# Mamba-2 SSD, two chunks: the second chunk's inter-chunk part from scores against the first chunk, instead of from a state

## The chip, the cores and the metric

The kernel runs on one core of a Trainium2 chip. The core has engines with a queue of instructions each: TensorE (PE; its weight loads are shown as PEld), VectorE (DVE), ScalarE (ACT), GpSimd (POOL) and SyncE (SP, which here only issues DMAs). The metric is the device time of one execution in microseconds (us), lower is better. A profile shows one execution of the program, recorded by the hardware.

## What is computed

The program is one decoder layer over 256 tokens of width 1024: a SwiGLU block, a mixer, another SwiGLU block. The mixer runs a Mamba-2 SSD branch and a retention branch side by side. The change lies in the SSD branch alone. Cut to it:

```python
CHUNK = 128                                   # 256 tokens: two chunks
SSD_N_HEADS, SSD_N_GROUPS = 32, 4             # 8 heads share B and C of a group
SSD_HEAD_DIM, SSD_D_STATE = 64, 128

def ssd_branch(z, xbc, dt_raw, ...):
    ...
    xdt = xs * dt[..., None]
    cb = jnp.einsum('bclgn,bcsgn->bgcls', cm, bm)
    scores = cb[:, :, None] * segsum_exp(a)
    y_diag = jnp.einsum('bgrcls,bcsgrp->bclgrp', scores, xdt)
    decay_to_end = jnp.exp(a_cs[..., -1:] - a_cs)
    chunk_states = jnp.einsum('bclgn,bgrcl,bclgrp->bcgrpn', bm, decay_to_end, xdt)
    chunk_decay = jnp.exp(a_cs[..., -1])
    prev_states = exclusive_chunk_scan(jnp.moveaxis(chunk_states, 1, 0), ...)
    y_off = jnp.einsum('bclgn,cbgrpn,bgrcl->bclgrp', cm, prev_states, jnp.exp(a_cs))
    y = y_diag + y_off + xs * d_skip.reshape(g_, r_)[..., None]
    ...
```

With two chunks only the second one has a `y_off`, and its `prev_states` is the state that the first chunk leaves behind.

## The kernel before

Activations lie transposed, features on the 128 partitions and the 256 tokens along the row. All weights come from memory in 1 MB stages (`wst`, four buffers, issued by SP in program order as buffers come free). Each stage is split into a rounded high half and the remainder: ACT casts the high half (L137), DVE subtracts (L138), into a ring of four buffers (`wh`). A projection multiplies high by high, high by low and low by high (`mm3`, L148 to L154), all in the reduced type f32r; these make nearly all of PE's work. The small products inside the branches are plain f32, which the trace shows as two instructions for each product and as one for each transpose.

The mixer is a list of steps, `ORDER` (L55), carried out in turn as program order. A planner takes this order as priority and lays the queue of each engine from its own estimates of durations; on DVE, ACT and SP neighbouring steps therefore mix. The SSD steps, for each of four groups `g`:

- `conv.8` to `conv.11` give B and C of all groups, `bT` and `cT` (state dimension on the partitions, tokens along the row). `conv.0` to `conv.7` give the inputs `xs`. The last `conv` in the order is `conv.3`.
- `bc` (`bc_products`, L658), once. Four transposes (L661) turn the first chunk's B; ACT copies them to `bn` (L662). Then eight products of 128 columns (L669), for each group and chunk that chunk's B against the same chunk's C; DVE multiplies them by the triangle and writes `cbm` (L672).
- `ml.g` (`mask_rows`) broadcasts the cumulated decays by POOL's DMAs into `m` and `ec`; `ma.g`, `mb.g` (`ssd_masks`) turn them into exponentials on ACT.
- `states.g` (`ssd_states`, L695) transposes `xs` (L700), scales it by dt into `xd` (L701), and scales the first chunk by its decay to the chunk's end into `xe` (L706).
- `mul.g` (`mask_scores`, L741) multiplies the masks by `cbm` (L743).
- `state.g` (`ssd_state`, L711) multiplies `bn` and `xe` to the state of the group, 128 x 512 (L715), and ACT copies it to `st` (L716).
- `back.g` (`ssd_back`, L746) does the products within chunks (L754), adds the skip (L760), then multiplies `st` by the second chunk's C (L764), scales by `ec` (L766) and adds (L767).

`v.p`, `z.g.p`, `bs.g.p`, `norma.g` and `normb.g` between them are projections and norms of the same mixer. PSUM tiles of the small products come from four buffers (`misc_ps`), those of projections from four others (`proj_ps`); each is one bank.

`xe`, `st` and `bn` are single buffers of 128 x 512, `ec` has two. In the retention part behind, `ret_scores` (L878) uses the same four names again for its decay masks, which SP loads (L881) when the buffer comes free.

Of the kernel before, what the change touches and what calls it, by code (L numbers as in the profile page):

```python
# [16 lines left out]
ALU = mybir.AluOpType  # L17

P = 128
T = 256  # L20
# [33 lines left out]

ORDER = (  # L55
# [27 lines left out]
def layer(ctx: ExitStack, tc: tile.TileContext, a, out, packing):  # L83
    nc = tc.nc
    pe, act, dve = nc.tensor, nc.scalar, nc.vector
# [12 lines left out]
    def nm(s):  # L98
        uid[0] += 1
        return f"{s}_{uid[0]}"  # L100

    def proj_ps():
        return pp.tile([P, 2, T], F32, tag="proj", name=nm("proj"))

    def misc_ps():
        return pm.tile([P, 512], F32, tag="misc", name=nm("misc"))
# [13 lines left out]
    def load(w, r0, nk, c0, ncol):  # L120
        st = stage()[:, :nk * ncol]
        fetch(st, w, lambda m: m[r0:r0 + nk * P, c0:c0 + ncol].reshape(nk, P, ncol)
              .transpose(1, 0, 2))
        return st.rearrange("p (k n) -> p k n", k=nk)
# [42 lines left out]
    ident = head[:, H_ID:H_ID + P]  # L167
    triu = k[:, K_TRI:K_TRI + P]
# [186 lines left out]
    with (tc.tile_pool(name="ep", bufs=1) as ep,  # L355
# [34 lines left out]
        for i in range(2):  # L390
# [8 lines left out]
            for f in range(2 - i):  # L399
                for tt in range(2):  # L400
                    pe.matmul(stat[:, tt * P:(tt + 1) * P], sq[:, f, tt * P:(tt + 1) * P], mean1,
                              start=i == f == tt == 0, stop=i == tt == 1, skip_group_check=True)
# [53 lines left out]
        ps = misc_ps()  # L456
        for c in range(2):
            pe.matmul(ps[:, c * P:(c + 1) * P], r[:, c:c + 1].broadcast_to([P, P]), ident,
                      start=True, stop=True)
# [84 lines left out]
    with tc.tile_pool(name="mx", bufs=1, reuse_waits="tile") as mx:  # L544
        def slot(shape, dt=F32, name="s"):
            return mx.tile(shape, dt, tag="slot", name=nm(name), bufs=SLOTS)
# [4 lines left out]
        def small(shape, tag, bufs=1):  # L551
            return mx.tile(shape, F32, tag=tag, name=nm(tag), bufs=bufs)
# [5 lines left out]
        bT, cT = slot([P, 4, T]), slot([P, 4, T])  # L558
# [84 lines left out]
        def silu_half(key, c0, p2):  # L643
            need("s")
            if p2 == 0:
                zs[key] = slot([P, 4, T])
            if key == ("z", 0):
                for f in range(4):
                    lookup(zs[key][:, f, :], first[f][0], AF.Silu, bias=first[f][1])
                return  # L650
            ps = pair_project(w_in, c0 + p2 * 256, u)
            lookup(zs[key][:, 2 * p2:2 * p2 + 2, :], ps, AF.Silu)

        bn = small([P, 512], "bn").rearrange("p (g n) -> p g n", g=4)
        cs, dend = small([P, 2, NH], "cs"), small([P, NH], "dend")
        cbs, states, masks = [], {}, {}

        def bc_products():  # L658
            ps = misc_ps()
            for g in range(4):  # L660
                pe.transpose(ps[:, g * P:(g + 1) * P], bT[:, g, :P], ident)  # L661
            act.copy(bn, ps.rearrange("p (g n) -> p g n", g=4))  # L662
            cbm = slot([P, 4, 2, P])
            for g2 in range(2):
                ps = misc_ps()
                for gg in range(2):
                    for c in range(2):
                        g = g2 * 2 + gg
                        pe.matmul(ps[:, (gg * 2 + c) * P:(gg * 2 + c + 1) * P],  # L669
                                  bT[:, g, c * P:(c + 1) * P], cT[:, g, c * P:(c + 1) * P],  # L670
                                  start=True, stop=True)
                dve.tensor_tensor(cbm[:, g2 * 2:g2 * 2 + 2].rearrange("p g c l -> p (g c) l"),  # L672
                                  ps.rearrange("p (a l) -> p a l", a=4),
                                  triu.unsqueeze(1).broadcast_to([P, 4, P]), ALU.mult)
            cbs.append(cbm)

        def decays():
# [30 lines left out]
                dend[:, 8 * g:8 * g + 8].unsqueeze(2).broadcast_to([P, 8, 64]), ALU.mult)  # L708
            states[g] = xd, xe

        def ssd_state(g):  # L711
            xd, xe = states[g]
            st = small([P, 512], "st")
            ps = misc_ps()
            pe.matmul(ps, bn[:, g, :], xe, start=True, stop=True)  # L715
            act.copy(st, ps)  # L716
            states[g] = xd, st

        def mask_rows(g):
            ec = small([P, 512], "ec", 2)  # L720
            m = [wide([P, 8, P]) for _ in range(2)]
            masks[g] = ec, m
            for c in range(2):
                nc.gpsimd.dma_start(m[c], rows[c:c + 1, 8 * g:8 * g + 8, :].broadcast_to([P, 8, P]))
            for hh in range(2):
                src = rows[1:2, 8 * g:8 * g + 8, :].rearrange("o (i two) l -> two o i l", two=2)[hh]
                nc.gpsimd.dma_start(ec[hh * 64:hh * 64 + 64, :].rearrange("p (i l) -> p i l", i=4),
                                    src.broadcast_to([64, 4, P]))

        def ssd_masks(g, c):  # L730
            need("e")
            ec, m = masks[g]
            for hl in range(8):
                hd = 8 * g + hl
                act.activation(m[c][:, hl, :], m[c][:, hl, :], AF.Relu,
                               bias=cs[:, c, hd:hd + 1], scale=-1.0)
            lookup(m[c], m[c], AF.Exp, scale=-1.0)
            if c == 1:
                lookup(ec, ec, AF.Exp)
# [4 lines left out]
                                  cbs[0][:, g, c, :].unsqueeze(1).broadcast_to([P, 8, P]), ALU.mult)  # L744

        def ssd_back(g):  # L746
            (xd, st), (ec, m) = states.pop(g), masks.pop(g)
            for f2 in range(2):
                py = misc_ps()
                for f in range(2):  # L750
                    for hh in range(2):
                        hl = (f2 * 2 + f) * 2 + hh
                        for c in range(2):
                            pe.matmul(py[hh * 64:hh * 64 + 64, f * T + c * P:f * T + (c + 1) * P],  # L754
                                      xd[:, c, hl * 64:hl * 64 + 64], m[c][:, hl, :],
                                      start=True, stop=True)
                for f in range(2):
                    ff = f2 * 2 + f
                    i = 4 * g + ff
                    dve.scalar_tensor_tensor(xs[g][:, ff, :], xs[g][:, ff, :], dskip[:, i:i + 1],  # L760
                                             py[:, f * T:(f + 1) * T], ALU.mult, ALU.add)
            po = misc_ps()
            for f in range(4):
                pe.matmul(po[:, f * P:(f + 1) * P], st[:, f * P:(f + 1) * P], cT[:, g, P:],  # L764
                          start=True, stop=True)
            dve.tensor_tensor(ec, ec, po, ALU.mult)  # L766
            dve.tensor_tensor(xs[g][:, :, P:], xs[g][:, :, P:],  # L767
                              ec.rearrange("p (f l) -> p f l", f=4), ALU.add)
# [139 lines left out]
        def ret_norm(hd):  # L908
# [14 lines left out]

        steps = {
            "dt": dt_tile, "conv": conv, "decays": decays, "bc": bc_products,
            "z": lambda g, p2: silu_half(("z", g), C_Z + g * 512, p2),
            "g": lambda g, p2: silu_half(("g", g), C_G + g * 512, p2),
            "states": ssd_states, "state": ssd_state,
            "ma": lambda g: ssd_masks(g, 0), "mb": lambda g: ssd_masks(g, 1), "ml": mask_rows,
            "mul": mask_scores, "back": ssd_back, "norma": norm_a,  # L930
            "normb": norm_b, "v": v_tile, "bs": lambda g, q: branch("s", "w_br_ssd", g, q),
            "br": lambda g, q: branch("r", "w_br_ret", g, q),
# [31 lines left out]
    with tc.tile_pool(name=nm("fp"), bufs=1, reuse_waits="tile") as fp:  # L964
# [5 lines left out]
        for p2 in range(NF // 2):  # L970
# [14 lines left out]
            if p2 == 5:  # L985
                g = sp.tile([P, KD], F32, tag="g", name=nm("g"), bufs=2)
# [4 lines left out]
                for q in range(2):  # L991
                    ps = misc_ps()
                    pe.matmul(ps, ones, diag[:, 4 * q:4 * q + 4, :].rearrange("p f t -> p (f t)"),
                              start=True, stop=True)
                    act.copy(gb[:, q * 512:(q + 1) * 512], ps)
            if p2 == 6:
                for tt in range(2):
                    for q in range(2):
                        ps = misc_ps()
# [17 lines left out]
        for bi in range(2):  # L1017
            c0, per, split = bi * 512, 4, NF - 6 if bi else NF
            ps = [proj_ps().rearrange("p f t -> p (f t)") for _ in range(2)]
# [6 lines left out]
            for k0 in range(0, NF, per):  # L1026
                kn = min(per, NF - k0)
                st = load("ffn2_w_out", k0 * P, kn, c0, 512)
# [82 lines left out]
```

## Time and profile before

| what | value |
|---|---|
| device time, median of 3 runs | 828.91 us (828.78 to 828.99) |
| device time of the profiled execution | 828.89 us |
| its span, first to last instruction | 826.8 us |
| instructions | 15886 |
| mean granted TensorE clock | 0.998 |
| DMA | 193.08 MB, 234 GB/s on the mean |
| first and last start of `bc`'s products (L661, L669) | 275.9 and 278.0 us |
| first and last start of the state products (L715) | 290.0 and 370.7 us |
| last start of L764 | 396.1 us |

Times inside a profile count from the span's start. A line such as L715 is the line of the kernel that issued the instruction. "Busy" is the share of the span in which an engine had an instruction under way. In the chain of the work that ended last, each piece of time is given to the instruction that the end waited for. A wait names what the engine was released by. Matmuls of PE are pipelined: the duration shown for one is longer than the distance to the next.

### The profile page before, as it was taken

Reading aid. Unit: us, or ns where it says so; the run is one execution under the profiler, and the core shown is the slowest. Engines: PE = TensorE matmul, PEld = TensorE weight load, DVE = VectorE, ACT = ScalarE, POOL = GpSimd, SP = SyncE. Lnnn points to the kernel's source line nnn. Section 1 sums busy time; section 2 is a strip of 40 time slices with the busy share of each in tenths; the row PEclk is TensorE's granted clock in tenths of the full one; section 3 lists DMA queues with packets and bytes.
Section 4 is the critical chain, followed back from the end, with each engine's and each line's share of the span. In section 5 each row is a group of like instructions: output and inputs, shape, how many; then the busy total and the mean of one; then the engine's idle time right before and its main releaser. Section 6 shows DMA issues by size and latency. Waiting matters only on the chain.

```text
span 826.8 us, 15886 instructions
## 1 busy us (share of the span) xinstructions
PE 816.1 (99%) x6612; PEld 787.0 (95%) x6612; DVE 666.9 (81%) x999; ACT 511.0 (62%) x731; POOL 10.3 (1%) x21
## 2 busy tenths in 40 slices
PE   8999999999999999999999999999999999999996
PEld 7999999999999989999999999999999999999885
DVE  7999899977989988787898778977979985455464
ACT  6566454556898777765565569765568754545342
POOL 0000000000200010000000000000000000000000
PEclk9999999999999999999999999999999999999999
DMA  9998899855685465546657754654565695455521
GB/s 367 415 418 344 314 349 366 335 180 173 233 309 200 158 216 187 200 130 239 229 182 301 254 205 153 211 198 171 212 218 183 255 360 185 176 185 185 206 87 52
DMA packets 30299, 193.08 MB, mean 234 GB/s; under 512 B 3458, under 2 KB 4098, under 8 KB 9619
## 3 DMA queue, kind: packets, MB, share of 16 engines
q1 hardware_dynamic: 28370, 186.07, 61.6%
q0 software_dynamic: 1568, 5.28, 1.9%
q8 instruction: 52, 0.85, 0.4%
q10 hardware_dynamic: 288, 0.72, 0.3%
q14 instruction: 21, 0.16, 0.1%
HBM read 190.97 MB, written 1.08 MB: 232 GB/s over the span
## 4 chain that ended last, share of the span: by engine, by line
PE 90%; ACT 3%; DVE 3%; DMA 3%; issue 1%; SPq 0%; ACTq 0%
PE proj L154 25%; PE proj L153 25%; PE proj L152 25%; PE proj L149 2%; PE proj L150 2%; PE proj L148 2%; DMA wst<-in_ffn_w_in_dram 2%; ACT wh L411 1%; DMA ada<-in_ada_w_dram 1%; PE misc L754 1%; PE misc L898 1%; PE misc L223 1%; DVE wh L414 1%; DVE wh L138 1%; DVE ada L197 1%; PE misc L764 1%
## 5 line engine op out<-in xcount | busy, mean ns | idle before, releaser
L138 DVE TENSOR_TENSOR wh<-wst,wh 128x1024 fp32r<-128x1024 f32 (+1 forms) x262 | 316.8, 1213 | 108.4 <-ACT wh L137 107.5
L137 ACT CAST wh<-wst 128x1024 fp32r<-128x1024 f32 (+1 forms) x262 | 272.4, 1042 | 171.0 <-PE proj L154 132.2
L152 PE MATMUL proj<-uh,wh 128*128 128x256 f32 (+1 forms) x1096 | 304.5, 278 | 0.0
L153 PE MATMUL proj<-ul,wh 128*128 128x256 f32 (+1 forms) x1096 | 303.2, 277 | 0.0
L154 PE MATMUL proj<-uh,wh 128*128 128x256 f32 (+1 forms) x1096 | 303.2, 277 | 0.0
L153 PEld LDWEIGHTS proj<-ul,wh 128*128 128x128 f32 x1096 | 205.8, 188 | 0.4 <-issue 0.2
L152 PEld LDWEIGHTS proj<-uh,wh 128*128 128x128 f32 x1096 | 205.8, 188 | 0.3 <-ACT wh L137 0.2
L154 PEld LDWEIGHTS proj<-uh,wh 128*128 128x128 f32 x1096 | 205.8, 188 | 0.2 <-issue 0.2
L152 PE MATMUL proj<-s,wh 128*128 128x256 f32 x312 | 87.1, 280 | 0.2 <-ACT s L142 0.2
L154 PE MATMUL proj<-s,wh 128*128 128x256 f32 x312 | 86.4, 277 | 0.0
L153 PE MATMUL proj<-s,wh 128*128 128x256 f32 x312 | 86.2, 277 | 0.0
L152 PEld LDWEIGHTS proj<-s,wh 128*128 128x128 f32 x312 | 58.5, 188 | 0.6 <-ACT s L142 0.4
L153 PEld LDWEIGHTS proj<-s,wh 128*128 128x128 f32 x312 | 58.6, 188 | 0.2 <-issue 0.2
L154 PEld LDWEIGHTS proj<-s,wh 128*128 128x128 f32 x312 | 58.6, 188 | 0.0
L197 DVE SCALAR_TENSOR_TENSOR ada<-ada,cb 128x1024 f32<-128x1024 f32 x48 | 57.3, 1219 | 0.0
L148 PE MATMUL proj<-uh,wh 128*128 128x256 f32 x152 | 42.0, 276 | 0.0
L149 PE MATMUL proj<-uh,wh 128*128 128x256 f32 x152 | 42.0, 276 | 0.0
L150 PE MATMUL proj<-ul,wh 128*128 128x256 f32 x152 | 42.0, 276 | 0.0
L152 PE MATMUL proj<-ah,wh 128*128 128x256 f32 x152 | 42.0, 276 | 0.0
L153 PE MATMUL proj<-al,wh 128*128 128x256 f32 x152 | 42.0, 276 | 0.0
L154 PE MATMUL proj<-ah,wh 128*128 128x256 f32 x152 | 42.0, 276 | 0.0
L186 ACT ACTIVATE s<-proj 128x512 f32<-128x512 f32 x33 | 19.7, 598 | 34.6 <-PE proj L154 32.5
(274 smaller groups left out, 1372.8 us busy)
## 6 DMA issues: line engine op xcount, KB each, us to landing
wst<-in_mix_w_in_dram SPq DMA_DIRECT2D x52, 1024.0 KB, 4.9
wst<-in_ffn_w_in_dram SPq DMA_DIRECT2D x43, 1024.0 KB, 5.5
wst<-in_ffn_w_out_dram SPq DMA_DIRECT2D x18, 1024.0 KB, 4.9
ada<-in_ada_w_dram SPq DMA_DIRECT2D x16, 1024.0 KB, 8.4
wst<-in_ada_w_dram SPq DMA_DIRECT2D x12, 1024.0 KB, 5.0
ada<-in_ada_w_dram SPq DMA_DIRECT2D x16, 512.0 KB, 12.6
wst<-in_w_br_ssd_dram SPq DMA_DIRECT2D x8, 1024.0 KB, 5.0
wst<-in_w_br_ret_dram SPq DMA_DIRECT2D x8, 1024.0 KB, 4.9
```

The source lines that it names most:

```text
L137: act.copy(hi, v)
L138: dve.tensor_tensor(lo, v, hi.bitcast(F32), ALU.subtract)
L148: pe.matmul(o, l[1], r[0], start=False, stop=False, skip_group_check=skip)
L149: pe.matmul(o, l[0], r[0], start=False, stop=False, skip_group_check=skip)
L150: pe.matmul(o, l[0], r[1], start=False, stop=False, skip_group_check=skip)
L152: pe.matmul(o, l[0], r[0], start=first, stop=False, skip_group_check=skip)
L153: pe.matmul(o, l[0], r[1], start=False, stop=False, skip_group_check=skip)
L154: pe.matmul(o, l[1], r[0], start=False, stop=last, skip_group_check=skip)
L186: phase["uses"].append(act.activation(*args, **kw).ins)
L197: dve.scalar_tensor_tensor(st[:, i, :], st[:, i, :], 1.0, cb, ALU.mult, ALU.mult, accum_out=raw[:, j, f0 + i:f0 + i + 1])
L223: pe.matmul(ps[:, :T], mean, s, start=i == 0, stop=i == len(parts) - 1)
L411: act.copy(hw[0][j], wst[kt][:, j, :])
```

## The change

The state of the first chunk is no longer formed. For the second chunk, the sum over the state dimension is done first: `bc` multiplies the first chunk's B by C of both chunks in one product of 256 columns per group. Its first half is masked as before; its second half, unmasked, is copied by ACT to `ahead` (in the buffer and under the tag that `bn` had). The products of the second chunk's B with its own C are done in four more products of 128 columns. `back.g` then multiplies `xe` by `ahead` where it multiplied `st` by C. The transposes of B, their copy, the steps `state.g` and their copies are gone; the other steps keep their order.

```diff
 ORDER = (
...
-    "conv.7 conv.5 conv.3 ma.0 bc v.0 mb.0 states.0 mul.0 v.1 state.0 back.0 ml.2 v.2 ma.1 v.3 "
-    "states.1 mb.1 norma.0 v.4 state.1 normb.0 mul.1 z.1.0 z.1.1 back.1 ml.3 states.2 bs.0.0 state.2 "
-    "ma.2 norma.1 bs.0.1 mb.2 v.5 normb.1 mul.2 z.2.0 z.2.1 v.6 back.2 states.3 bs.1.0 state.3 ma.3 "
+    "conv.7 conv.5 conv.3 ma.0 bc v.0 mb.0 states.0 mul.0 v.1 back.0 ml.2 v.2 ma.1 v.3 "
+    "states.1 mb.1 norma.0 v.4 normb.0 mul.1 z.1.0 z.1.1 back.1 ml.3 states.2 bs.0.0 "
+    "ma.2 norma.1 bs.0.1 mb.2 v.5 normb.1 mul.2 z.2.0 z.2.1 v.6 back.2 states.3 bs.1.0 ma.3 "
...
-        bn = small([P, 512], "bn").rearrange("p (g n) -> p g n", g=4)
+        ahead = small([P, 512], "bn").rearrange("p (g l) -> p g l", g=4)
...
         def bc_products():
-            ps = misc_ps()
-            for g in range(4):
-                pe.transpose(ps[:, g * P:(g + 1) * P], bT[:, g, :P], ident)
-            act.copy(bn, ps.rearrange("p (g n) -> p g n", g=4))
             cbm = slot([P, 4, 2, P])
             for g2 in range(2):
                 ps = misc_ps()
                 for gg in range(2):
-                    for c in range(2):
-                        g = g2 * 2 + gg
-                        pe.matmul(ps[:, (gg * 2 + c) * P:(gg * 2 + c + 1) * P],
-                                  bT[:, g, c * P:(c + 1) * P], cT[:, g, c * P:(c + 1) * P],
-                                  start=True, stop=True)
-                dve.tensor_tensor(cbm[:, g2 * 2:g2 * 2 + 2].rearrange("p g c l -> p (g c) l"),
-                                  ps.rearrange("p (a l) -> p a l", a=4),
-                                  triu.unsqueeze(1).broadcast_to([P, 4, P]), ALU.mult)
+                    g = g2 * 2 + gg
+                    pe.matmul(ps[:, gg * T:(gg + 1) * T], bT[:, g, :P], cT[:, g, :],
+                              start=True, stop=True)
+                ps = ps.rearrange("p (g c l) -> p g c l", g=2, c=2)
+                dve.tensor_tensor(cbm[:, g2 * 2:g2 * 2 + 2, 0, :], ps[:, :, 0, :],
+                                  triu.unsqueeze(1).broadcast_to([P, 2, P]), ALU.mult)
+                act.copy(ahead[:, g2 * 2:g2 * 2 + 2, :], ps[:, :, 1, :])
+            ps = misc_ps()
+            for g in range(4):
+                pe.matmul(ps[:, g * P:(g + 1) * P], bT[:, g, P:], cT[:, g, P:],
+                          start=True, stop=True)
+            dve.tensor_tensor(cbm[:, :, 1, :], ps.rearrange("p (g l) -> p g l", g=4),
+                              triu.unsqueeze(1).broadcast_to([P, 4, P]), ALU.mult)
             cbs.append(cbm)
...
-        def ssd_state(g):
-            xd, xe = states[g]
-            st = small([P, 512], "st")
-            ps = misc_ps()
-            pe.matmul(ps, bn[:, g, :], xe, start=True, stop=True)
-            act.copy(st, ps)
-            states[g] = xd, st
...
         def ssd_back(g):
-            (xd, st), (ec, m) = states.pop(g), masks.pop(g)
+            (xd, xe), (ec, m) = states.pop(g), masks.pop(g)
...
             for f in range(4):
-                pe.matmul(po[:, f * P:(f + 1) * P], st[:, f * P:(f + 1) * P], cT[:, g, P:],
+                pe.matmul(po[:, f * P:(f + 1) * P], xe[:, f * P:(f + 1) * P], ahead[:, g, :],
                           start=True, stop=True)
...
-            "states": ssd_states, "state": ssd_state,
+            "states": ssd_states,
```

## The prediction

> **What bounds the kernel now.** I start with the page: busy time of each engine (part 1), then its chain of the work that ended last (part 4).
>
> ```profile
> PE 816.1 (99%) x6612; PEld 787.0 (95%) x6612; DVE 666.9 (81%) x999; ACT 511.0 (62%) x731; POOL 10.3 (1%) x21
> ...
> PE 90%; ACT 3%; DVE 3%; DMA 3%; issue 1%; SPq 0%; ACTq 0%
> ```
>
> PE (TensorE's matmuls) is busy for 99% of the span and makes 90% of the chain. Since matmuls are pipelined, "busy" alone proves little, so the next view is the list of waits of PE, over the whole run:
>
> ```profile
> PE misc L389 <- DMA crow<-in_c_dram: 2.6, 1, 2.6
> PE misc L898 <- DVE m L889: 0.6, 1, 0.6
> PE proj L442 <- ACT wh L411: 0.4, 1, 0.4
> PE proj L152 <- ACT s L142: 0.2, 1, 0.2
> ```
>
> Columns: total us, times, longest. Asked for 270 to 400 us alone, where the SSD steps that the diff touches lie, the same list is empty; L898 is in the retention part behind them. So a microsecond of PE work taken out of the SSD steps should move everything behind it forward. Whether the feeders could follow is read from windows over these steps. The columns are length, then busy us of PE, PEld, DVE, ACT, POOL, then granted clock, share and rate of the DMA.
>
> ```profile
> 276.00:283.60 7.60, 7.60 (x45) 6.61 (x44) 6.50 (x14) 4.31 (x7) 0.00 (x0) 1.00 0.51 169
> 279.00:300.00 21.00, 21.00 (x123) 17.15 (x122) 18.47 (x25) 15.06 (x23) 2.35 (x4) 1.00 0.53 176
> 300.00:340.00 40.00, 40.00 (x305) 36.69 (x304) 32.70 (x43) 32.47 (x54) 1.79 (x3) 1.00 0.55 189
> 340.00:390.00 50.00, 50.00 (x382) 46.38 (x381) 40.09 (x54) 32.28 (x39) 0.00 (x0) 1.00 0.55 191
> ```
>
> PE fills each window at full clock (1.00). From 279 to 390 us DVE is idle for 2.5 + 7.3 + 9.9 = 19.7 us, and ACT for more: room for a change of a few microseconds, though not much in the first window.
>
> **The change, part by part.** What a step costs on PE is read from the chain in order of time (start, us, what), because the chain puts pipelined matmuls end to end. An f32 product appears as two instructions (x16 for the eight products of L669); a transpose as one.
>
> ```profile
> 276.08 0.44 PE misc L661 x4
> 276.52 1.79 PE misc L669 x16
> ...
> 290.12 0.86 PE misc L715 x2
> ...
> 292.92 1.09 PE misc L764 x8
> ...
> 311.28 0.86 PE misc L715 x2
> ...
> 332.64 0.86 PE misc L715 x2
> ...
> 370.43 0.86 PE misc L715 x2
> ...
> 483.69 0.43 PE misc L886 x2
> ...
> 499.59 0.70 PE misc L898 x2
> ```
>
> *Removed on PE.* The four transposes of B: 0.44 us. The eight 128-column products of `bc`: 1.79. The four `state` products (one per group, 512 columns): 4 x 0.86 = 3.44. Together 5.67 us.
>
> *Added on PE.* Four f32 products of 256 columns (first chunk's B against C of both chunks) and four of 128 columns (second chunk). The 256-column price is L886, same types, same width: 0.43 us each, so 1.72. For 128 columns half of the L669 row: 1.79 / 2 = 0.90. Together 2.62 us. As many columns are streamed as L669 and the transposes streamed; `bc` alone gets 2.62 - 2.23 = 0.39 us longer.
>
> *Net on PE: 5.67 - 2.62 = 3.05 us less.* The ends of this term: the first 256-column product of a group may cost 0.70, like the first L898 (0.27 more), and the eight 128-column instructions 1.09, like L764 (0.19 more), which leaves 2.59 us of saving. On the other side stands the 0.7 us that the weight loads of L764 idle in four times without a named releaser: if that was `st` after all, the saving is 3.75. I do not take it, because `st` of group 0 is written at 291.56 + 0.59 = 292.15, before L764 begins:
>
> ```profile
> 291.56 0.59 ACT L716 COPY st<-misc 128x512 f32<-128x512 f32 x1
> ...
> 292.85 0.97 PEld L764 LDWEIGHTS misc<-s,st 128*128 128x128 f32 x8 [0.17 <-issue]
> ...
> PEld misc L764 <- issue: 0.7, 4, 0.2
> ```
>
> *Cross-check by start times*, group 0. The timeline gives starts:
>
> ```profile
> 289.73 0.39 PE L154 MATMUL proj<-wh,ul 128*128 128x512 f32 x1
> 289.96 1.02 PE L715 MATMUL misc<-xe,bn 128*128 128x512 f32 x2
> ...
> 290.90 2.02 PE L754 MATMUL misc<-m,s 128*64 128x128 f32 x32
> ...
> 360.68 0.39 PE L154 MATMUL proj<-wh,ul 128*128 128x512 f32 x1
> 361.00 2.02 PE L754 MATMUL misc<-m,s 128*64 128x128 f32 x32
> ```
>
> From the last projection to the first L754 take 290.90 - 289.73 = 1.17 us with the state product between; in group 2, where `state` doesn't stand there, 361.00 - 360.68 = 0.32. Difference 0.85, against 0.86 in the chain.
>
> *What is late next in that place.* With `state.0` gone and `bc` 0.39 longer, L754 of group 0 starts at 290.90 - 0.85 + 0.39 = 290.44. It needs the masked scores of `mul.0`:
>
> ```profile
> 286.48 2.36 DVE L743 TENSOR_TENSOR m<-m,s 128x1024 f32<-128x1024 f32 x2
> ```
>
> They are done at 288.84, so 1.6 us remain. The product with `xe` (L764, unchanged in number and shape) now reads `xe`, which DVE writes before `mul.0`, and `ahead`, written in `bc`: both long there. In the order string `states.1` follows `back.0`, and so on, so that the single `xe` buffer, now held until L764, delays nobody.
>
> *ACT and DVE.* Groups of instructions by shape, with total us and mean ns:
>
> ```profile
> L662 ACT COPY bn<-misc 128x512 f32<-128x512 f32 x1 | 0.6, 568 | 0.0
> ...
> L716 ACT COPY st<-misc 128x512 f32<-128x512 f32 x4 | 2.3, 584 | 0.0
> ...
> L832 ACT ACTIVATE s<-proj,col 128x256 f32<-128x256 f32 x8 | 3.4, 472 | 6.7 <-PE proj L154 6.7
> ...
> L672 DVE TENSOR_TENSOR s<-misc,k 128x512 f32<-128x512 f32 x2 | 1.4, 679 | 0.0
> ...
> L281 DVE TENSOR_TENSOR misc<-misc,rs 128x256 f32<-128x256 f32 x4 | 1.7, 426 | 0.0
> ```
>
> ACT loses 0.57 + 4 x 0.58 = 2.9 us and gets two 256-column copies at about 0.47: 1.96 us less. DVE has 2 x 0.68 = 1.36 and gets 2 x 0.43 + 0.68 = 1.54: 0.18 more. I cost both at nothing: PE covers them, as it covers these engines' idle time above. If the cover were gone, DVE's 0.18 would be the price.
>
> *The added wait.* In `bc` DVE and ACT now read two halves of the same PSUM bank. The kernel already has that case: in a conv pair both halves of the bank are read by ACT (L571) and DVE (L574).
>
> ```profile
> L571 ACT ACTIVATE cv<-proj,col 128x256 f32<-128x256 f32 x24 | 13.3, 570 | 5.2 <-DVE cv L574 4.3 <-PE proj L154 0.9
> ```
>
> ACT waited there for DVE for 4.3 us in all, though the halves differ: the two readers are kept apart. So each copy to `ahead` will stand behind DVE's multiply of its bank, and behind it on ACT the last conv pair's activations and casts. From 276 to 283.6 ACT is idle for 7.60 - 4.31 = 3.3 us, which takes 2 x 0.47 - 0.57 = 0.37 us more and a wait. The Trainium skill, "PSUM — Partial Sum Buffer", section "PSUM bank collisions raise a hardware error", speaks against this part of the change: ScalarE and VectorE may not touch one bank's quadrant at once, two reads included. By that rule two readers gain nothing over one, and the first rival holds; the trace agrees with the 4.3 us.
>
> *Queues.* No DMA is added. The retention mask loads (L881) reuse `xe`, `st`, `bn`. `xe` and `bn` now come free after the last L764 instead of the last L715, `st` at once. SP already waits in this place:
>
> ```profile
> 374.92 0.43 SPq L881 DMA_DIRECT2D bn<-in_dmask_dram  x1
> ...
> 396.42 0.33 SPq L881 DMA_DIRECT2D st<-in_dmask_dram  x1
> 396.84 0.38 SPq L118 DMA_DIRECT2D wst<-in_mix_w_in_dram  x1
> ...
> SPq L881 <- PE misc L764: 5.7, 1, 5.7
> ```
>
> SP held the next weight load for 5.7 us and PE shows no wait behind it. Two mask loads in place of one there cost about 0.4 us of SP time (0.33 to 0.43 each): nothing on PE. POOL's mask broadcasts (released by L754) come earlier with it.
>
> **Sum.** The profiled execution took 828.89 us (span 826.8 and 2.1 around it), 0.02 below the median of 828.91. 828.89 - 3.05 = **825.8 us** (-0.37%). Behind the SSD steps every wait of PE hangs on something that PE releases, so the 3 us should arrive.
>
> **The rivals.**
>
> *ACT held behind DVE in `bc`.* For it: the L571 row, and DVE busy for 6.50 of 7.60 us around `bc`. Were DVE to reach its second multiply only at the end of that backlog, 283.6, ACT's copies end at 284.5, and the exponentials for `mul.0` slip. Against: ACT has 3.3 us idle, `mul.0` has 1.6 us slack. It decides from a hold of about 1.6 us on `mul.0`; a hold of 2.6 us gives back 1.0: 826.8.
>
> *The queues behind are laid differently.* The order on DVE and ACT comes from a planner with its own estimates, and taking instructions out may change it far away. The place where this would bite is the one behind with a PE wait, L898 at 499 us, fed by ACT then DVE.
>
> ```profile
> L197 DVE SCALAR_TENSOR_TENSOR wst<-wst,cb 128x1024 f32<-128x1024 f32 x24 | 29.0, 1220 | 0.8 <-DMA wst<-in_ada_w_dram 0.8
> ...
> L178 ACT ACT_TABLE_LOAD x30 | 38.5, 1283 | 1.2 <-PEq L1080 0.7
> ```
>
> One pair of L197 moved ahead of L889 delays PE by 2 x 1.22 = 2.4 us: 828.89 - 3.05 + 2.44 = 828.3, no change to be seen. Against: both orders follow the same step list.
>
> *Slower.* The same place at a higher price: two pairs of L197 (4.88) and a table load (1.28) on the path ahead of L889 make 6.2 us, and 828.89 - 3.05 + 6.16 = 832.0. It decides from 3.05 + 1.66 = 4.7 us of added wait. Against: the wait there is 0.6 us today, and no other step is renamed or moved.
>
> **How the numbers follow.** About 0.2% (1.66 us) is what can be told from no change here. Forecast 825.8, chance 0.72, own range 825.1 (saving 3.75) to 826.3 (2.59), and a little either way for the rest of the order. ACT held behind DVE, 826.8: 0.09. Queues laid differently, 828.3: 0.12. Slower, 832.0: 0.07. The range 825.0 to 827.3 holds the first two, 0.81. Faster by over 0.2% are the first two: 0.81; same 0.12; slower 0.07.
>
> **What would show it.** Right: no L715 row; the chain's `bc` rows sum to about 2.6 us with eight instructions of 256 columns; PE's waits between 270 and 480 us still absent; the last L764 starts about 3 us earlier, and the matmuls of the end too. The first rival shows as a wait of PE's L754 for DVE or ACT in group 0; the others as a longer wait at L898, or new ones further on. The forecast is wrong if the 256-column products take clearly more than 0.43, or if a PE wait above a microsecond appears anywhere behind.

## The result and the profile after

The changed kernel took 826.08 us (median of 6 runs, 825.60 to 826.34), the kernel before 828.85 us (828.66 to 828.99): a ratio of 0.9966 with a 95% interval of 0.9954 to 0.9977, about 2.8 us less. Forecast were 825.8. The profiled execution took 825.60 us, with a span of 823.4.

The page of the changed kernel, busy time of each engine and the chain that ended last:

```profile
PE 812.7 (99%) x6600; PEld 785.3 (95%) x6600; DVE 666.5 (81%) x1000; ACT 508.7 (62%) x728; POOL 10.3 (1%) x21
...
PE 88%; DVE 4%; ACT 3%; DMA 3%; issue 1%; SPq 0%; ACTq 0%
```

PE is busy for 3.4 us less and still for 99% of the span. Of its list of waits (total us, times, longest) these are the three longest. Lines behind the change have moved by seven, so L891 is the former L898, with the wait of before; new is the wait of L442 for ACT's L430, in the first 50 us of the program. From 270 to 480 us the list is empty, as before:

```profile
PE misc L389 <- DMA crow<-in_c_dram: 2.3, 1, 2.3
PE misc L891 <- DVE m L882: 0.6, 1, 0.6
PE proj L442 <- ACT uh L430: 0.6, 1, 0.6
```

The chain in order of time (start, us, what) shows the shift grow step by step. L664 and L672 are the products of `bc`, L747 the former L754, L757 the former L764, L879 the former L886:

```profile
276.25 1.73 PE misc L664 x8
277.98 0.89 PE misc L672 x8
...
290.67 1.95 PE misc L747 x32
292.62 1.09 PE misc L757 x8
...
322.09 1.95 PE misc L747 x32
...
358.95 1.95 PE misc L747 x32
...
390.35 1.95 PE misc L747 x32
...
480.69 0.43 PE misc L879 x2
```

`bc` takes 1.73 + 0.89 = 2.62 us. Against the profile before, `bc` begins 0.17 later (276.25 for 276.08). The four L747 begin 0.31, 1.19, 2.12 and 3.00 earlier (before: 290.98, 323.28, 361.07 and 393.35): after the first one, each step is the missing state product, 0.88 to 0.93. From there the shift stays, 3.00 at the first retention scores (480.69 for 483.69). Some 0.3 us more come in between there and the end of the retention part, where ACT's pair of activations ahead of the merge starts at 609.72 instead of 613.06; why was not followed up.

So far everything is as forecast. What did not fit was the spread: 0.74 us between the six runs of the changed kernel, 0.33 between those of the kernel before beside them.

### The profile page after: what moved, and what is told of

It is laid out like the page before. It is cut to its first block, busy times and chain, and to the rows that moved or that the text cites. A ratio compares the mean times of both kernels' runs of the same rounds, so it can differ in the third digit from the quotient of the medians.

```text
span 823.4 us, 15854 instructions
## 1 busy us (share of the span) xinstructions
PE 812.7 (99%) x6600; PEld 785.3 (95%) x6600; DVE 666.5 (81%) x1000; ACT 508.7 (62%) x728; POOL 10.3 (1%) x21
## 4 chain that ended last, share of the span: by engine, by line
PE 88%; DVE 4%; ACT 3%; DMA 3%; issue 1%; SPq 0%; ACTq 0%
PE proj L154 25%; PE proj L153 25%; PE proj L152 25%; PE proj L150 2%; PE proj L149 2%; PE proj L148 2%; DMA wst<-in_ffn_w_in_dram 2%; ACT wh L411 1%; DMA ada<-in_ada_w_dram 1%; PE misc L747 1%; DVE wh L138 1%; PE misc L891 1%; DVE ada L197 1%; DVE wh L414 1%; PE misc L223 1%
## 5 line engine op out<-in xcount | busy, mean ns | idle before, releaser
L186 ACT ACTIVATE s<-proj 128x512 f32<-128x512 f32 x33 | 19.7, 597 | 34.1 <-PE proj L154 31.8
```

The lines of the kernel that those rows point to most:

```text
L186: phase["uses"].append(act.activation(*args, **kw).ins)
```

## The experiments

Two theories stood at the start. **PE's work**: the gain is the 3.05 us that PE no longer does. **Another engine or queue**: it is ACT's lost copies, or the new order of the queues and the earlier load into `st`. A third one came out of the first runs.

### The products put back, without the copies (e1)

```diff
-    "conv.7 conv.5 conv.3 ma.0 bc v.0 mb.0 states.0 mul.0 v.1 back.0 ml.2 v.2 ma.1 v.3 "
+    "conv.7 conv.5 conv.3 ma.0 bc v.0 mb.0 states.0 mul.0 v.1 state.0 back.0 ml.2 v.2 ma.1 v.3 "
...
+        def ssd_state(g):
+            xd, xe = states[g]
+            ps = misc_ps()
+            pe.matmul(ps, ahead[:, g, :], xe, start=True, stop=True)
```

> The changed kernel with four idle products of 512 columns (first chunk's scores against xe, into a PSUM tile that nobody reads) at the places where the state products stood; no copy by ACT. If the gain is PE's work alone, the four products cost 4 x 0.86 = 3.44 us again: 826.08 + 3.44 = 829.5. If the gain came from the copies that ACT lost, or from the order of the queues and the earlier mask load, they cost nothing: 826.1.

Measured: 829.16 us (828.76 to 830.63, 11 runs), ratio to the kernel before 1.0005 (0.9996 to 1.0014). The chain of e1 has the four products again:

```profile
290.78 0.86 PE misc L715 x2
...
311.94 0.86 PE misc L715 x2
...
333.31 0.86 PE misc L715 x2
...
371.10 0.86 PE misc L715 x2
```

Matmuls that nobody reads give back the whole gain: 3.1 us above the 826.08, 3.5 above the 825.70 of the repeat below, for 3.44 expected (both on other chips; on its own chip e1 is 0.2 us slower than the kernel before, where 0.39 us of longer `bc` are left). That is PE's work, and speaks against the other theory. Of the 1.9 us between e1's lowest and highest run only 0.6 lie within the span (826.8 to 827.4); what the rest outside it is was not tried.

### The copies put back, without the products (e2, twice)

```diff
-    ... mul.0 v.1 back.0 ...
+    ... mul.0 v.1 state.0 back.0 ...
...
+        def ssd_state(g):
+            xd, xe = states[g]
+            act.copy(small([P, 512], "st"), xe)
```

> The changed kernel with four copies of 128x512 on ACT, xe to st, at the places where ACT copied the state; no product on PE. The buffer st is thereby held again until late, so that its mask load moves back too. If the gain is PE's work alone: 826.1, no change against the changed kernel. If it came from ACT: 4 x 0.58 = 2.3 us more, 828.4. If it came from the early mask load: above 826.1 by what that was worth.

Measured: 827.08 us (825.74 to 828.47, 11 runs), 0.9980 (0.9971 to 0.9989). Inconclusive: the lowest run is what PE's work gives, the highest what ACT's copies would cost, and the profiled run (826.27) has no wait of PE in the SSD steps.

### The kernel before, without the products (e5)

```diff
-            ps = misc_ps()
-            pe.matmul(ps, bn[:, g, :], xe, start=True, stop=True)
-            act.copy(st, ps)
+            act.copy(st, xe)
```

> The kernel before without its four state products: ACT copies xe to st in their place, so the second chunk's inter-chunk part is left wrong by the missing product with B. Transposes, bc, copies and buffers as before. If PE's work alone counts: 828.85 - 3.44 = 825.4. If it is ACT's copies that counted: 828.9.

Measured: 826.71 us (825.96 to 828.04, 11 runs), 0.9976 (0.9967 to 0.9984): 2.2 us of 3.44, with a wide spread again. Here the profile has the missing part. First the wait of PE, then its chain:

```profile
PE misc L223 <- DVE sql L776: 1.0, 1, 1.0
```

```profile
307.43 0.95 ACT wh L137
308.40 1.23 DVE wh L138
309.63 0.67 DVE s L701 x2
310.30 0.44 issue
310.74 0.68 DVE xe L706
311.43 0.35 DVE sql L776
311.81 0.38 PE misc L223
```

PE stands for 1.0 us before the norm's sum (L223), because ACT and DVE are late: with the state product gone, PE arrives earlier than they do. Why they are late is read from what ACT waits for; e5's chain itself shows mask activations between the casts and goes back from there to PE (at 302.65 us), not to the rows. The list of ACT's waits from 276 to 420 us, before and then after the change (L728 is the former L735, the first mask activation):

```profile
ACT m L735 <- DMA m<-rows: 4.0, 2, 3.0
```

```profile
ACT m L728 <- DMA m<-rows: 6.8, 2, 5.5
```

The planner has queued mask activations of later groups early on ACT, and there they stand for the broadcast of the mask rows, with weight casts and PSUM evacuations in order behind them. Each line sums two waits. The first ends near 300 us, 3.0 us long before the change and 5.5 now. The second ends near 329 us; before the change it was 1.0 long:

```profile
329.71 1.57 ACT L735 ACTIVATE m<-m,cs 128x128 f32<-128x128 f32 x5 [1.00 <-DMA m<-rows]
```

Hence a third theory, **ACT held by the mask rows**: PE's work gives the gain, and executions in which the rows land late give part of it back.

### The same kernel again, and the mask activations held back (a_again, e6)

```diff
-        act.copy(hi, v)
+        last["cast"] = act.copy(hi, v).ins
...
+            with tc.issue_after(last["cast"]) if g >= 2 else nullcontext():
                 for hl in range(8):
...
                     act.activation(m[c][:, hl, :], m[c][:, hl, :], AF.Relu,
```

> The changed kernel as it is, on the chip of the three kernels beside it. PE's work alone: 825.8, with the spread of the kernel before (some 0.6 us between lowest and highest). If a wait on ACT for the mask rows (5.5 us in the profile) now sometimes reaches PE: the same lowest time, but a spread of 1 us or more and a median above 826.

> The changed kernel; the mask activations of groups 2 and 3 may not be queued on ACT ahead of the weight cast that precedes them in the step list, so that ACT's casts no longer stand behind a wait for the mask rows' DMA. If that wait eats part of the gain in some executions: median 825.4 to 825.8 and a spread of 0.6 us or less. If PE's work alone decides: the same median and spread as the changed kernel, about 826.0.

Measured on one chip: the changed kernel 825.70 us (825.62 to 825.85, 5 runs), e6 825.60 us (825.54 to 825.68, 5 runs), the kernel before 828.77; 0.9964 (0.9951 to 0.9977) and 0.9962 (0.9949 to 0.9975). ACT's timeline in e6 (start, us, engine, line; in brackets what ended its idle time) has no wait for the rows; casts come with PE, the mask activations in one piece of eight:

```profile
297.89 1.05 ACT L139 CAST wh<-wst 128x1024 fp32r<-128x1024 f32 x1 [3.73 <-PE proj L156]
...
319.11 2.44 ACT L731 ACTIVATE m<-m,cs 128x128 f32<-128x128 f32 x8
```

The spread falls from 0.23 to 0.14 us. But the changed kernel's spread was small on this chip too, which by the expectation of a_again speaks for PE's work alone; e6 fits both of its answers. This pair alone decides nothing.

### One reader for each bank (e3), and the order within `back` (e4)

The edit of e3, in place of the products of `bc`:

```diff
+            for bc_, cc in ((0, 0), (0, 1), (1, 1)):
+                ps = misc_ps()
+                for g in range(4):
+                    pe.matmul(ps[:, g * P:(g + 1) * P], bT[:, g, bc_ * P:(bc_ + 1) * P],
+                              cT[:, g, cc * P:(cc + 1) * P], start=True, stop=True)
+                ps = ps.rearrange("p (g l) -> p g l", g=4)
+                if bc_ == cc:
+                    dve.tensor_tensor(cbm[:, :, cc, :], ps, ..., ALU.mult)
+                else:
+                    act.copy(ahead, ps)
```

> The changed kernel, with the products of bc laid into three PSUM banks that have one reader each: DVE for the first chunk's scores, ACT for those ahead, DVE for the second chunk's; twelve products of 128 columns. PE's work alone: 24 x 0.112 = 2.69 instead of 2.62 us, no difference. If ACT's wait behind DVE in a shared bank costs time: faster by up to 0.4 us.

> The changed kernel; in each back step the products of xe with the scores ahead (L757) are issued before the 64-column products within the chunks (L747) instead of behind them. The switch between them idles the weight loads for 0.17 us in each group: if that idle time hangs on the order, up to 4 x 0.2 = 0.8 us less, 825.3; if the switch costs the same either way round, no difference.

e3 took 825.94 us (825.52 to 826.97, 6 runs), 0.9967 (0.9955 to 0.9980): no gain. Its chain gives `bc` as one row, twelve products of 128 columns:

```profile
276.18 2.68 PE misc L663 x24
```

2.68 for 2.62 us: at these sizes the columns cost, and hardly how many products they are cut into (twelve instead of eight). And e3's profiled run, one of its slower ones (826.69 us), shows by accident what the third theory says. Its wait of PE, and its chain at that place (L723 is the mask activation, L808 the evacuation of a projection, L742 the products within chunks of groups 1 and 2):

```profile
PE proj L152 <- ACT s L808: 0.7, 1, 0.7
```

```profile
322.08 1.95 PE misc L742 x32
...
324.53 5.48 DMA m<-rows
330.09 1.57 ACT m L723 x5
331.66 0.48 ACT s L808
...
360.02 1.95 PE misc L742 x32
```

PE waits for a PSUM buffer, its evacuation stands behind mask activations on ACT, and these stand for the rows.

The edit of e4:

```diff
             (xd, xe), (ec, m) = states.pop(g), masks.pop(g)
+            po = misc_ps()
+            for f in range(4):
+                pe.matmul(po[:, f * P:(f + 1) * P], xe[:, f * P:(f + 1) * P], ahead[:, g, :],
+                          start=True, stop=True)
             for f2 in range(2):
...
-            po = misc_ps()
-            for f in range(4):
-                pe.matmul(po[:, f * P:(f + 1) * P], xe[:, f * P:(f + 1) * P], ahead[:, g, :],
-                          start=True, stop=True)
```

Measured: 825.70 us (825.43 to 826.54, 5 runs), 0.9964 (0.9951 to 0.9977), no difference. Its chain, then that of a_again for the same stretch:

```profile
285.00 0.87 PE misc L701 x8
291.34 0.89 PE misc L743 x8
292.23 1.95 PE misc L751 x32
305.30 0.87 PE misc L701 x8
...
325.63 1.02 PE misc L701 x8
```

```profile
284.36 0.87 PE misc L701 x8
...
304.65 0.88 PE misc L701 x8
```

The products of `xe` are cheaper (0.89 for 1.09), but what follows the 64-column ones then pays (the L701 at 325.63, 1.02 for 0.87). From one L701 to the next are 20.30 us here and 20.29 there: the cost of the switch only moves.

### The third theory on the noisy kernels (e7, e8, e9)

e7 is e2 and e9 is e5, each with the mask activations held back as in e6; e8 is the kernel before with that edit alone. e2 ran beside e7 again, and the changed kernel beside e9.

> The changed kernel with ACT's four copies put back and no product, as in e2, beside the next run on the same chip. As in e2: lowest about 825.8, median about 827, spread above 2 us.

> As e2 with the four copies on ACT, and the mask activations of groups 2 and 3 held behind the preceding weight cast, as in e6. If the loss and the spread of e2 come from ACT standing before the mask rows' DMA with weight casts and evacuations behind it: 825.6 to 825.8, spread below 0.6 us. If ACT's 2.3 us of copies cost time by themselves: as e2, about 827.

> The kernel before, with the mask activations of groups 2 and 3 held behind the preceding weight cast. If the kernel before has slack enough for the wait, as its small spread suggests: no change, 828.7 to 828.9. If the gain of the changed kernel came from another order of these activations: faster by up to 3 us.

> As e5, the kernel before without its four state products (the second chunk's inter-chunk part lacks the product with B), and with the mask activations of groups 2 and 3 held behind the preceding weight cast. If the 1.0 us wait of PE in e5 and its spread come from the order behind the mask rows' DMA: 828.85 - 3.44 = 825.4, spread below 0.6 us. If the four products also hid the latency of the norm between them: as e5, about 826.7.

> The changed kernel once more, beside e9. As before: lowest about 825.6, median 825.7 to 826.1, spread 0.2 to 1 us.

| kernel | median us | lowest to highest | runs | ratio to before, 95% interval |
|---|---|---|---|---|
| e2_again, copies back | 826.48 | 825.64 to 830.81 | 12 | 0.9978, 0.9968 to 0.9988 |
| e7, the same with masks held back | 825.33 | 825.22 to 825.75 | 5 | 0.9958, 0.9946 to 0.9969 |
| e8, kernel before with masks held back | 828.86 | 828.58 to 829.04 | 11 | 0.9999, 0.9990 to 1.0007 |
| e9, e5 with masks held back | 825.18 | 825.09 to 825.28 | 5 | 0.9956, 0.9942 to 0.9970 |
| a_third, the changed kernel | 826.21 | 825.54 to 826.67 | 5 | 0.9968, 0.9955 to 0.9980 |

With the masks held back ACT's four copies cost nothing (e7), and the missing products bring nearly all of their 3.44 us (e9: 3.6 less than the 828.80 of the kernel before beside it, of which 3.2 lie within the span, 823.4 for 826.6). The spread goes from 2 us and more, in 11 or 12 runs, to 0.5 and 0.2, in 5 each. The same edit does nothing to the kernel before (e8), which has the slack. All three came out against the other answer of each; e8 and e9 as the third theory expected, e7 0.3 us below its range. Some 0.2 of that lie outside the span: e7's median span, 823.4, is that of the fastest runs of the changed kernel. e5 ran on another chip than e9, and the edit moves the mask activations as well as the wait, so this pair doesn't tell the cost of the wait from that of the activations ahead of the casts.

The profiled run of a_third (826.05 us) has the rows in the changed kernel's own chain:

```profile
322.04 1.95 PE misc L747 x32
...
324.49 4.86 DMA m<-rows
329.43 1.57 ACT m L728 x5
331.00 0.48 ACT s L813
...
359.32 1.95 PE misc L747 x32
```

For comparison the timeline of the first profile of the changed kernel, 825.60 us, with the issue of the rows on POOL and the first activation behind it, and the same of a_again, 825.85 us:

```profile
324.54 0.56 POOL L717 DMA_DIRECT2D m<-rows  x1 [26.31 <-DVE s L753]
...
328.87 1.58 ACT L728 ACTIVATE m<-m,cs 128x128 f32<-128x128 f32 x5 [1.36 <-DMA m<-rows]
```

```profile
324.56 0.56 POOL L717 DMA_DIRECT2D m<-rows  x1 [25.64 <-DVE s L753]
...
329.10 1.58 ACT L728 ACTIVATE m<-m,cs 128x128 f32<-128x128 f32 x5 [1.57 <-DMA m<-rows]
```

The rows are issued at the same time in all four executions (324.5), and ACT starts at 328.87, 329.10, 329.43 and 330.09 (the last in e3); their times are 825.60, 825.85, 826.05 and 826.69. The later the rows, the longer the execution, by nearly the same amount. And PE loses it in this place: from the products within chunks of group 1 to those of group 2 (L747 of the changed kernel) the chain has 36.86, 37.13, 37.28 and 37.94 us, and 36.86 in e6, 36.87 in e7, 36.86 in e9, where ACT doesn't wait for the rows. In a_again and a_third PE's list of waits has nothing there; only these starts show the loss.

Not every slow execution is of this kind. e4's profiled run is its slowest (826.54 us) and has 36.85 us there; its `bc` begins 0.67 us later than that of the first profile (276.92 for 276.25), and it has two waits of PE for DVE at L401 in the first 50 us, 0.7 us together, that the others lack. e2's profiled run (826.27) has 37.03. The highest runs of the changed kernel and of e2_again (826.67 and 830.81) have no profile.

## Why the prediction was right

*PE bounds the SSD steps.* Right: e1 gives the gain back with idle products, e9 takes it in the kernel before by leaving the products out.

*The sum on PE.* Right. `bc` measured 2.62 us for 2.62, and the 5.67 us that went stood in the rows of before. The net of 3.05 came out as 3.17 by the shift of the last L747 (3.00, and the 0.17 by which `bc` began later), as 3.07 between the medians of a_again and its kernel before, and as 2.8 in the result.

*What is late next.* Right in its place: L754 of group 0 was set at 290.44; in the timeline it starts at 290.60 (as L747), in an execution that was 0.17 later throughout. `mul.0` held nothing up.

*The added wait in `bc`.* It exists, and is covered. The second copy in the timeline after the change:

```profile
279.19 0.37 ACT L669 COPY bn<-misc 128x256 f32<-128x256 f32 x1 [0.35 <-DVE s L667]
```

It waits 0.35 us for DVE's multiply of the same bank. e3, where no bank has two readers, is no faster. So the first rival did not come about, and neither did the other two, which would have shown at L891.

*The mask loads.* As forecast: `st` is loaded early, `xe` and `bn` after the last L757 (SP's queue in the timeline), and PE waits for none of them.

```profile
204.60 0.42 SPq L874 DMA_DIRECT2D st<-in_dmask_dram  x1
...
393.42 0.33 SPq L874 DMA_DIRECT2D xe<-in_dmask_dram  x1
...
394.28 0.43 SPq L874 DMA_DIRECT2D bn<-in_dmask_dram  x1
```

*Where it fell short.* The step "I cost both at nothing: PE covers them" judged the feeders by their idle time, of which ACT had even more than the 19.7 us of DVE. But an idle ACT is not a free one: it stood for the mask rows with PE's casts and evacuations behind it, in two waits of 3.0 and 1.0 us that the list of ACT's waits showed before the change, and that were not read. The same holds for "POOL's mask broadcasts (released by L754) come earlier with it", costed at nothing. In the changed kernel the longer wait grew to 5.5 us and costs PE nothing: from the first L747 to the second are 31.42 us in all three of its profiles. It is the short one, 1.4 to 2.0 us now, that reaches PE in some executions, for 0.27 us in a_again and 0.42 in a_third, against the first profile. That the slower runs, up to 826.67, lost more in the same way is likely but not shown. The first rival had the right engine, held behind another; it named the wrong place and releaser.

*What was luck.* The 826.08 lie within the prediction's own range, but its upper end of 826.3 was reckoned from dearer products, and `bc` was not dearer. The forecast also lacked the 0.3 us that came in behind the first retention scores, which offset part of what the rows took.

e6 keeps the gain in every run, 825.60 us beside 825.70 for the changed kernel on its chip, a difference too small to tell. That it would also keep it on the chips where the changed kernel took 826.08 and 826.21 is argued from e7 and e9; e6 ran on one chip.

## What to carry to other kernels

On a PE that hardly waits, a change's worth is the sum of chain rows on PE; here it could be had to some tenths of a microsecond. Before adding it up, read for each feeding engine not its idle share but what it stands for in order, and what is queued behind that: such a wait cost nothing here until PE got three microseconds faster. A spread that grows with a change can be the sign of a wait that has become nearly late; here the profile of one slower execution, and holding back the waiting instructions, found it.

## What the runs showed of the hardware

The broadcast of the mask rows, issued at 324.5 us by POOL in four executions of nearly the same program, let ACT start 4.3 to 5.6 us later. What sets that time was not tried. The broadcast near 293 us took longer in the changed kernel as well (issued at 292.87 instead of 293.18, ACT's start at 299.90 instead of 297.60); a weight load goes out shortly before it in both, 1.6 us ahead after the change and 2.6 before, but that the two get in each other's way is only argued. An ACT copy of 128x256 out of PSUM took 0.37 us, where an activation with a bias of that size had 0.47 at L832 and 0.57 at L571.
